# Shorter GpSimd operations, a first group without GpSimd arithmetic, later row sums and a separate bank in the last group, in a one-core decoder trunk step

## The chip, the cores and the metric

The kernel runs on one core of one Trainium2 chip. A core has five engines that run their own instruction queues and wait for one another by semaphores: TensorE (PE, matmuls, with PEld for its weight loads), VectorE (DVE), ScalarE (ACT), GpSimd (POOL) and SyncE (SP, which issues the transfers here). The metric is the device time of one execution in microseconds; a kernel's number is the median of its runs.

## The reference

One layer of a decoder trunk for 256 prompt tokens and 32 sample tokens (8 sequences of 4), T = 288 tokens in all, D = 2048 channels, float32:

```python
h = rmsnorm(x, norm1_g)
proj = h @ w_in + b_in                      # 2048 -> 3072: a, gate, z of 1024 each
u = a * sigmoid(gate)
c = silu(layernorm(depthwise_causal_conv([history, u], conv_w) + conv_b))   # 31 taps
d = window_mean([history, z], windows 2, 4, 8, 16) - z                       # one window per group of 256
p = (d @ pool_w, group by group) * pool_scale
x = x + concat(c, p) @ w_out
h2 = rmsnorm(x, norm2_g)
x = x + square(relu(h2 @ w_ff1)) @ w_ff2    # 2048 -> 8192 -> 2048
y = rmsnorm(x, norm_f)
```

The last 30 rows of u and the last 15 rows of z are outputs as well.

## The kernel before

Channels lie on the 128 partitions, the 288 tokens along the free dimension. Every weight block of 1024 x 256 values (1 MB, tile `wr`, three buffers) is loaded by SyncE and split by `split` into two halves of 128 x 1024 values; each half becomes a rounded part `whi` (ScalarE, L224) and a remainder `wlo` = wr - whi (L225, VectorE or GpSimd), with four buffers for each. The activations are split in the same way (`hx`, `dx`, `px`, `mx`, `ax`, `fx`). `gemm` multiplies in three matmuls for each k and each of two column blocks m: whi times high part (L247), whi times low part (L248), wlo times high part (L249), into `ac`, a tile of two PSUM banks, of which there are two.

Which engine makes a `wlo` is counted in eighths by `SHARE`: `turn` grows by the share of the stage at each half, and at eight the half goes to GpSimd. In the first group the halves are cut into two pieces of 128 x 512 columns (`cut=2`), in all others a piece is the whole half.

The stages are: a first group (`conv_products(0)`) for which also x is loaded and split into `hx` (L265 on ScalarE, L266 on VectorE); a second (`conv_products(1)`); five more conv groups; four pool groups (`pool_group`, windows 16, 8, 4, 2); the last conv group; then four small products with `pool_w`, the output projection over `px` (L450) and over `mx` (L459), and four rounds of the two feed-forward products (L494, L507). Each group of w_in has 96 matmuls.

The row sums of x squared are taken while the first group runs: GpSimd squares three pairs of channel blocks (L298), ScalarE five (L300), GpSimd adds (L302, L304). `rsqrt_sums` multiplies the totals by ones (`pt`, L186), takes the square root and its reciprocal; `spread` (`pr`, L204) brings it to all partitions and ScalarE copies it to `rb` (L391). In the second group's `gemm` the first is called at k = 3 and the second at k = 8.

`conv_pair` scales the product by `rb` (`ag`, L322), takes the sigmoid, writes u (L327) and then, at lowest priority (`later`), does 31 taps of the convolution one after another on VectorE, one operand in PSUM (`pc`, L337), with the sample tokens on GpSimd (`prd`, L340) and VectorE (L342); after every second channel block GpSimd adds into `sum_c` (L345, L347). `pool_group` scales (`tz`, L358), forms window sums on GpSimd by doubling (`s`, L366, 840 columns at a time), and the differences on VectorE (L369, L374, L378, L379, `dx` L382).

The order of the instructions on each engine is fixed before the run: the framework takes the program's order as priority and lets each engine take the first instruction that is ready by its own estimate of the times.

In the last feed-forward product the final group is computed with `m_outer=True`, first all k of m = 0, then all of m = 1; its product is added to x (L507), squared (L512) and added to the row sum `ssf` (L514), before the last normalisation (L524).

Of the kernel before, what the change touches and what calls it, by code (L numbers as in the profile page):

```python
# [9 lines left out]
F32 = mybir.dt.float32  # L10
F32R = mybir.dt.float32r
AF = mybir.ActivationFunctionType
ALU = mybir.AluOpType
# [4 lines left out]
D = 2048  # L18
SEQ = 256
NB, NS = 8, 4  # L20
T = SEQ + NB * NS
# [59 lines left out]
def trunk_kernel(ctx: ExitStack, tc: tile.TileContext, io):  # L81
# [18 lines left out]
    def nm(s):  # L100
        seen[s] = seen.get(s, 0) + 1
        return f"{s}{seen[s]}"
# [109 lines left out]

    def split(raw, share=0, cut=4):

        parts = []
        for h in range(2):
            hi = wspl.tile([P, 4, 256], F32R, name=nm("whi"), tag="whi")
            lo = wspl.tile([P, 4, 256], F32R, name=nm("wlo"), tag="wlo")
            turn["n"] += share
            eng = nc.gpsimd if turn["n"] >= 8 else nc.vector  # L220
            turn["n"] %= 8
            for k in range(0, 4, cut):
                src = raw[:, 4 * h + k : 4 * h + k + cut, :]
                nc.scalar.copy(hi[:, k : k + cut, :], src)  # L224
                eng.tensor_tensor(lo[:, k : k + cut, :], src, hi[:, k : k + cut, :].bitcast(F32), op=ALU.subtract)  # L225
            parts.append((hi, lo))

        def get(k, m):
            hi, lo = parts[k // 4]
            return hi[:, k % 4, m * P : (m + 1) * P], lo[:, k % 4, m * P : (m + 1) * P]  # L230

        return get

    def gemm(banks, rhs, m_outer=False, between={}):


        n = len(rhs)
        gets = ready.pop()
        order = [(k, m) for k in range(n) for m in range(2)]
        if m_outer:  # L240
            order.sort(key=lambda km: km[1])
        for k, m in order:
            if m == 0 and k in between:
                between[k]()
            (xh, xl), b = rhs[k], banks[:, m, :T]
            wh, wl = gets[k // 8](k % 8, m)
            nc.tensor.matmul(b, wh, xh, start=k == 0, stop=False)  # L247
            nc.tensor.matmul(b, wh, xl, start=False, stop=False)  # L248
            nc.tensor.matmul(b, wl, xh, start=False, stop=k == n - 1)  # L249
        ready.extend(itertools.islice(weights, 1))  # L250

    def bank2():
        return acc.tile([P, 2, 512], F32, name=nm("ac"), tag="ac")

    def halves(x2):

# [32 lines left out]

    scratch = z_all[:].rearrange("p k t -> p (k t)")[:, 0 : 5 * 2 * T].rearrange("p (n k t) -> p n k t", n=5, t=T)  # L290
    tot = [scratch[:, 0], scratch[:, 1]]
    used = [False, False]
    for q in range(8):
        xq = xT[:, 2 * q : 2 * q + 2, :]
        a = 0 if q in (0, 2, 4) else 1
        dst = scratch[:, 2 if a == 0 else 3 + q % 2] if used[a] else tot[a]
        if a == 0:
            nc.gpsimd.tensor_tensor(dst, xq, xq, op=ALU.mult)  # L298
        else:
            nc.scalar.activation(dst, xq, AF.Square)  # L300
        if used[a]:
            nc.gpsimd.tensor_tensor(tot[a], tot[a], dst, op=ALU.add)  # L302
        used[a] = True
    nc.gpsimd.tensor_tensor(tot[1], tot[1], tot[0], op=ALU.add)  # L304
    rb = row("rb")


# [3 lines left out]
    def conv_products(i, **kw):  # L311
        nc.sync.dma_start(u_all[:, i, UO:UL], io["hist_c"][:, i, :])
        bk = bank2()
        gemm(bk, hx, **kw)
        return bk

    def conv_pair(i, bk):
        up = u_all[:, i, 0:UO]
        us = samples(u_all[:, i, UO:UL], US)
        ag = tmpp.tile([P, 2, T], F32, name=nm("ag"), tag="ag", bufs=2)  # L320
        ta, tg = ag[:, 0, :], ag[:, 1, :]
        nc.vector.tensor_tensor(ag, bk[:, :, :T], both(rb), op=ALU.mult)  # L322
        nc.scalar.activation(tg, tg, AF.Sigmoid, bias=v("b_in", 8 + i))
        if i == N8 - 1:
            load_table(AF.Sqrt, tg[:, 0:1])
        for out, a, b in ((up[:, CH:UO], ta[:, :SEQ], tg[:, :SEQ]), (us[:, :, CH:US], samples(ta[:, SEQ:T], NS), samples(tg[:, SEQ:T], NS))):
            nc.vector.scalar_tensor_tensor(out=out, in0=a, scalar=v("b_in", i), in1=b, op0=ALU.add, op1=ALU.mult)  # L327
        if i % 2 == 0:
            cs.append(actp.tile([P, 2, T], F32, name=nm("c"), tag="c", bufs=4))
        c = cs[i // 2][:, i % 2, :]  # L330
        with later():
            pc = cvp.tile([P, SEQ], F32, name=nm("pc"), tag="cv", padded_shape=[P, 512])
            cwv = vec[:, CWO + i * CW : CWO + (i + 1) * CW]
            nc.scalar.activation(pc, up[:, 0:SEQ], AF.Identity, bias=v("conv_b", i), scale=cwv[:, 0:1])
            for w in range(1, CW):
                dst = pc if w < CW - 1 else c[:, 0:SEQ]
                nc.vector.scalar_tensor_tensor(out=dst, in0=up[:, w : w + SEQ], scalar=cwv[:, w : w + 1], in1=pc, op0=ALU.mult, op1=ALU.add)  # L337
            prd = prdp.tile([P, NB, NS, CW], F32, name=nm("prd"), tag="prd", padded_shape=[P, NB, NS, CW])
            for t in range(NS):
                nc.gpsimd.tensor_tensor(prd[:, :, t, :], us[:, :, t : t + CW], cwv[:, None, :].to_broadcast([P, NB, CW]), op=ALU.mult)  # L340
            cso = c[:, SEQ:T]
            nc.vector.tensor_reduce(samples(cso, NS), prd, axis=AX.X, op=ALU.add)  # L342
            nc.scalar.activation(cso, cso, AF.Identity, bias=v("conv_b", i))
            if i == 3:
                nc.gpsimd.tensor_tensor(sum_c, cs[0], cs[1], op=ALU.add)  # L345
            elif i % 2 and i > 3:
                nc.gpsimd.tensor_tensor(sum_c, sum_c, cs[i // 2], op=ALU.add)  # L347


    dd = {}  # L350
# [1 line left out]
    def pool_group(g):  # L352
        nc.sync.dma_start(z_all[:, 2 * g : 2 * g + 2, ZO:ZL], io["hist_p"][:, 2 * g : 2 * g + 2, :])
        bk = bank2()
        gemm(bk, hx)
# [13 lines left out]
        nc.vector.scalar_tensor_tensor(  # L369
# [2 lines left out]
        for m in range(2):  # L372
# [10 lines left out]
        dd[g] = halves((dh, dl))  # L383

    first = conv_products(0)
    diag = []
    second = conv_products(
        1,
        between={
            3: lambda: diag.append(rsqrt_sums([tot[1][:, 0, :], tot[1][:, 1, :]], 1.0 / D, AF.Sigmoid)),  # L390
            8: lambda: nc.scalar.copy(rb, spread(diag[0])[:, :T]),  # L391
        },
    )
    nc.gpsimd.memset(z_all[:, :, 0:PH], 0.0)
# [12 lines left out]
    mixp = {}  # L407
    for g in GROUPS:
        bk = bank2()
        gemm(bk, dd[g])  # L410
        for m, (mh, ml) in enumerate(halves(act2("px"))):
            i = 2 * g + m
            nc.scalar.activation(mh, bk[:, m, :T], AF.Copy, scale=v("pool_scale", i))
            nc.vector.scalar_tensor_tensor(out=ml, in0=bk[:, m, :T], scalar=v("pool_scale", i), in1=f32(mh), op0=ALU.mult, op1=ALU.subtract)
            mixp[i] = (mh, ml)
# [29 lines left out]

    for g in range(8):
        bk = bank2()
        gemm(bk, [mixp[k] for k in korder])
        x2 = xT[:, 2 * g : 2 * g + 2, :]
        nc.vector.tensor_tensor(x2, x2, bk[:, :, :T], op=ALU.add)  # L450

# [2 lines left out]
    ss2 = row("ss2")  # L454
    for g in range(8):
        bk = bank2()
        gemm(bk, mixc)
# [26 lines left out]
    for ch in range(DFF // FCH):  # L484
        fx = []
        for g in range(FCH // 256):
            bk = bank2()
            gemm(bk, x1)
            if ch == 0 and g == 0:
                nc.scalar.copy(r2, rsqrt_rows([ss2, q2], 1.0 / D)[:, :T])  # L490
            t = tmpp.tile([P, 2, T], F32, name=nm("t"), tag="ag", bufs=2)
            nc.vector.scalar_tensor_tensor(out=t, in0=bk[:, :, :T], scalar=0.0, in1=both(r2), op0=ALU.max, op1=ALU.mult)
            f = tmpp.tile([P, 2, T], F32, name=nm("f"), tag="ag2", bufs=2)
            nc.scalar.activation(f, t, AF.Square)  # L494
            fh, fl = act2("fx")
            nc.scalar.copy(fh, f)
            nc.vector.tensor_tensor(fl, f, f32(fh), op=ALU.subtract)
            fx += halves((fh, fl))
        last = ch == DFF // FCH - 1
        for g in range(8):  # L500
            bk = bank2()
            gemm(bk, fx, m_outer=last and g == 7)
            for m in range(2):
                k = 2 * g + m
                xk = xT[:, k, :]
                if last:
                    nc.vector.tensor_tensor(xk, xk, bk[:, m, :T], op=ALU.add)  # L507
# [76 lines left out]
```

## Time and profile before

| | us |
|---|---|
| median of 3 runs (1132.56 to 1134.32) | 1134.06 |
| the profiled execution | 1131.78 |
| its span, first to last instruction | 1130.0 |
| TensorE busy | 1092.2 (97%) |
| VectorE busy | 657.0 (58%) |
| ScalarE busy | 468.6 (41%) |
| GpSimd busy | 190.0 (17%) |

Durations in the profile come from one execution. A row of a timeline gives start, duration, engine, line, operation, output and inputs, size and count, and in brackets the idle time before it and what ended it. A row of a group gives the count, the total busy time, the mean in ns, and the idle time before. An instruction that has begun but waits for a port counts as busy. The granted clock of TensorE has a mean of 0.986 over the execution.

### The profile page before, as it was taken

Reading aid. Unit: us, or ns where it says so; the run is one execution under the profiler, and the core shown is the slowest. Engines: PE = TensorE matmul, PEld = TensorE weight load, DVE = VectorE, ACT = ScalarE, POOL = GpSimd, SP = SyncE. Lnnn points to the kernel's source line nnn. Section 1 sums busy time; section 2 is a strip of 40 time slices with the busy share of each in tenths; the row PEclk is TensorE's granted clock in tenths of the full one; section 3 lists DMA queues with packets and bytes.
Section 4 is the critical chain, followed back from the end, with each engine's and each line's share of the span. In section 5 each row is a group of like instructions: output and inputs, shape, how many; then the busy total and the mean of one; then the engine's idle time right before and its main releaser. Section 6 shows DMA issues by size and latency. Waiting matters only on the chain.

```text
span 1130.0 us, 19074 instructions
## 1 busy us (share of the span) xinstructions
PE 1092.2 (97%) x8208; PEld 1086.9 (96%) x8208; DVE 657.0 (58%) x822; ACT 468.6 (41%) x575; POOL 190.0 (17%) x139
## 2 busy tenths in 40 slices
PE   5999995999999999999999999999999999999995
PEld 5999995999999999999999999999999999999995
DVE  7699999677854454444544444455444444454553
ACT  6444444365544443333444333344433334444441
POOL 7598985431300000000000000000000000000000
PEclk9999998899999999999999999999999999999997
DMA  7554536445444444444454545454445454545432
GB/s 278 177 182 154 182 115 175 152 150 186 152 162 171 161 176 160 176 159 178 154 182 156 180 155 182 153 184 153 183 153 184 153 183 152 184 151 185 152 112 84
DMA packets 31909, 187.00 MB, mean 165 GB/s; under 512 B 3408, under 2 KB 7760, under 8 KB 10448
## 3 DMA queue, kind: packets, MB, share of 16 engines
q1 hardware_dynamic: 31680, 185.73, 47.5%
q8 instruction: 64, 1.05, 0.4%
q14 instruction: 21, 0.17, 0.0%
q10 hardware_dynamic: 144, 0.05, 0.0%
HBM read 181.49 MB, written 4.28 MB: 164 GB/s over the span
## 4 chain that ended last, share of the span: by engine, by line
PE 91%; DVE 6%; ACT 0%; issue 0%; DVEq 0%; ACTq 0%
PE ac L247 31%; PE ac L248 30%; PE ac L249 30%; DVE pc L337 2%; DVE wlo L225 1%; PE pt L186 0%; DVE xT L524 0%; DVE d L369 0%; DVE d L374 0%; DVE e L378 0%; PE pr L204 0%; DVE d L379 0%; DVE dx L382 0%; DVE c L342 0%; DVE tz L358 0%
## 5 line engine op out<-in xcount | busy, mean ns | idle before, releaser
L224 ACT CAST whi<-wr 128x1024 fp32r<-128x1024 f32 (+1 forms) x342 | 355.2, 1040 | 577.6 <-PE ac L248 569.0
L225 DVE TENSOR_TENSOR wlo<-wr,whi 128x1024 fp32r<-128x1024 f32 (+1 forms) x295 | 367.9, 1247 | 349.1 <-ACT whi L224 348.1
L247 PE MATMUL ac<-ax,whi 128*128 128x288 f32 x1024 | 302.7, 296 | 0.0
L247 PE MATMUL ac<-fx,whi 128*128 128x288 f32 x1024 | 302.4, 295 | 0.0
L248 PE MATMUL ac<-fx,whi 128*128 128x288 f32 x1024 | 301.4, 294 | 0.0
L248 PE MATMUL ac<-ax,whi 128*128 128x288 f32 x1024 | 301.3, 294 | 0.0
L249 PE MATMUL ac<-ax,wlo 128*128 128x288 f32 x1024 | 298.1, 291 | 0.0
L249 PE MATMUL ac<-fx,wlo 128*128 128x288 f32 x1024 | 298.0, 291 | 0.0
L249 PEld LDWEIGHTS ac<-fx,wlo 128*128 128x128 f32 x1024 | 192.9, 188 | 0.0
L249 PEld LDWEIGHTS ac<-ax,wlo 128*128 128x128 f32 x1024 | 192.8, 188 | 0.0
L247 PEld LDWEIGHTS ac<-ax,whi 128*128 128x128 f32 x1024 | 192.2, 188 | 0.1
L247 PEld LDWEIGHTS ac<-fx,whi 128*128 128x128 f32 x1024 | 192.2, 188 | 0.0
L248 PEld LDWEIGHTS ac<-ax,whi 128*128 128x128 f32 x1024 | 192.0, 187 | 0.1
L248 PEld LDWEIGHTS ac<-fx,whi 128*128 128x128 f32 x1024 | 192.0, 187 | 0.0
L249 PE MATMUL ac<-hx,wlo 128*128 128x288 f32 x384 | 115.8, 302 | 12.4 <-DVE wlo L225 11.6
L225 POOL TENSOR_TENSOR wlo<-wr,whi 128x1024 fp32r<-128x1024 f32 (+1 forms) x47 | 112.4, 2402 | 51.0 <-ACT whi L224 50.8
L247 PE MATMUL ac<-hx,whi 128*128 128x288 f32 x384 | 115.8, 302 | 0.3 <-ACT whi L224 0.3
L248 PE MATMUL ac<-hx,whi 128*128 128x288 f32 x384 | 113.9, 297 | 0.0
L337 DVE SCALAR_TENSOR_TENSOR pc<-u_all,vec,pc 128x256 f32<-128x256 f32 x232 | 99.1, 482 | 3.5 <-issue 1.2
L249 PEld LDWEIGHTS ac<-hx,wlo 128*128 128x128 f32 x384 | 73.5, 191 | 14.3 <-DVE wlo L225 13.1
L247 PEld LDWEIGHTS ac<-hx,whi 128*128 128x128 f32 x384 | 73.9, 192 | 0.8 <-ACT whi L224 0.8
L248 PEld LDWEIGHTS ac<-hx,whi 128*128 128x128 f32 x384 | 73.8, 192 | 0.3
(111 smaller groups left out, 844.4 us busy)
## 6 DMA issues: line engine op xcount, KB each, us to landing
wr<-in_w SPq DMA_DIRECT2D x167, 1024.0 KB, 4.9
xT<-in_xT SPq DMA_DIRECT2D x8, 288.0 KB, 5.9
wr<-in_w SPq DMA_DIRECT2D x8, 256.0 KB, 5.7
out_u_out<-u_all SPq DMA_DIRECT2D x1, 1208.0 KB, 9.0
out_yT<-xT SPq DMA_DIRECT2D x2, 576.0 KB, 2.9
u_all<-in_hist_c SPq DMA_DIRECT2D x8, 136.0 KB, 4.8
out_z_out<-z_all SPq DMA_DIRECT2D x1, 668.0 KB, 8.9
z_all<-in_hist_p SPq DMA_DIRECT2D x4, 152.0 KB, 4.3
```

The source lines that it names most:

```text
L224: nc.scalar.copy(hi[:, k : k + cut, :], src)
L225: eng.tensor_tensor(lo[:, k : k + cut, :], src, hi[:, k : k + cut, :].bitcast(F32), op=ALU.subtract)
L247: nc.tensor.matmul(b, wh, xh, start=k == 0, stop=False)
L248: nc.tensor.matmul(b, wh, xl, start=False, stop=False)
L249: nc.tensor.matmul(b, wl, xh, start=False, stop=k == n - 1)
L337: nc.vector.scalar_tensor_tensor(out=dst, in0=up[:, w : w + SEQ], scalar=cwv[:, w : w + 1], in1=pc, op0=ALU.mult, op1=ALU.add)
```

## The change

Four edits. `SHARE["first"]` goes from 2 to 0, so that no `wlo` of the first group is made on GpSimd. Where GpSimd makes a `wlo`, it does so in pieces of two k-blocks, 512 columns; the window sums and the channel sums are cut into one operation for each m as well. The squares of x all go to ScalarE and their additions to VectorE, in program order behind the first group's product and the second group's weights, with two totals of two parts each that `pt` adds up; `pt` is called at k = 10 of the second group and the spread at k = 14. In the last group of the last product, m = 1 accumulates in a bank of another tile.

```diff
-SHARE = {"first": 2, "second": 4, "conv": 7, "pool": 5, "pool_w": 3, "w_out": 6}
+SHARE = {"first": 0, "second": 4, "conv": 7, "pool": 5, "pool_w": 3, "w_out": 6}
...
             turn["n"] += share
-            eng = nc.gpsimd if turn["n"] >= 8 else nc.vector
+            slow = turn["n"] >= 8
             turn["n"] %= 8
             for k in range(0, 4, cut):
                 src = raw[:, 4 * h + k : 4 * h + k + cut, :]
                 nc.scalar.copy(hi[:, k : k + cut, :], src)
-                eng.tensor_tensor(lo[:, k : k + cut, :], src, hi[:, k : k + cut, :].bitcast(F32), op=ALU.subtract)
+                eng, step = (nc.gpsimd, 2) if slow else (nc.vector, cut)
+                for j in range(k, k + cut, step):
+                    eng.tensor_tensor(lo[:, j : j + step, :], raw[:, 4 * h + j : 4 * h + j + step, :], hi[:, j : j + step, :].bitcast(F32), op=ALU.subtract)
...
-    used = [False, False]
-    for q in range(8):
-        xq = xT[:, 2 * q : 2 * q + 2, :]
-        a = 0 if q in (0, 2, 4) else 1
-        dst = scratch[:, 2 if a == 0 else 3 + q % 2] if used[a] else tot[a]
-        if a == 0:
-            nc.gpsimd.tensor_tensor(dst, xq, xq, op=ALU.mult)
-        else:
+
+    def squares():
+        for q in range(8):
+            xq = xT[:, 2 * q : 2 * q + 2, :]
+            a = q // 4
+            dst = scratch[:, 2 + q % 3] if q % 4 else tot[a]
             nc.scalar.activation(dst, xq, AF.Square)
-        if used[a]:
-            nc.gpsimd.tensor_tensor(tot[a], tot[a], dst, op=ALU.add)
-        used[a] = True
-    nc.gpsimd.tensor_tensor(tot[1], tot[1], tot[0], op=ALU.add)
+            if q % 4:
+                nc.vector.tensor_tensor(tot[a], tot[a], dst, op=ALU.add)
...
-            if i == 3:
-                nc.gpsimd.tensor_tensor(sum_c, cs[0], cs[1], op=ALU.add)
-            elif i % 2 and i > 3:
-                nc.gpsimd.tensor_tensor(sum_c, sum_c, cs[i // 2], op=ALU.add)
+            if i % 2 and i > 1:
+                for m in range(2):
+                    nc.gpsimd.tensor_tensor(sum_c[:, m, :], (cs[0] if i == 3 else sum_c)[:, m, :], cs[i // 2][:, m, :], op=ALU.add)
...
-            nc.gpsimd.tensor_tensor(s2[:, :, 2 * w - 1 :], s[:, :, 2 * w - 1 :], s[:, :, w - 1 : ZL - w], op=ALU.add)
+            for m in range(2):
+                nc.gpsimd.tensor_tensor(s2[:, m, 2 * w - 1 :], s[:, m, 2 * w - 1 :], s[:, m, w - 1 : ZL - w], op=ALU.add)
...
     first = conv_products(0)
+    squares()
     diag = []
     second = conv_products(
         1,
         between={
-            3: lambda: diag.append(rsqrt_sums([tot[1][:, 0, :], tot[1][:, 1, :]], 1.0 / D, AF.Sigmoid)),
-            8: lambda: nc.scalar.copy(rb, spread(diag[0])[:, :T]),
+            10: lambda: diag.append(rsqrt_sums([t[:, m, :] for t in tot for m in range(2)], 1.0 / D, AF.Sigmoid)),
+            14: lambda: nc.scalar.copy(rb, spread(diag[0])[:, :T]),
         },
     )
...
-            gemm(bk, fx, m_outer=last and g == 7)
+            banks = each(bk)
+            if last and g == 7:
+                banks[1] = bank2()[:, 1, :]
+            gemm(banks, fx, m_outer=last and g == 7)
...
-                    nc.vector.tensor_tensor(xk, xk, bk[:, m, :T], op=ALU.add)
+                    nc.vector.tensor_tensor(xk, xk, banks[m][:, :T], op=ALU.add)
```

More of the change, by code (lines that the diff above doesn't have):

```diff
@@ L253, in bank2, with each @@
         return acc.tile([P, 2, 512], F32, name=nm("ac"), tag="ac")
+    def each(bk):
+        return [bk[:, m, :] for m in range(2)]
     def halves(x2):
@@ L313, in conv_products @@
         bk = bank2()
-        gemm(bk, hx, **kw)
+        gemm(each(bk), hx, **kw)
         return bk
@@ L354, in pool_group @@
         bk = bank2()
-        gemm(bk, hx)
+        gemm(each(bk), hx)
         z = z_all[:, 2 * g : 2 * g + 2, :]
@@ L409, in trunk_kernel @@
         bk = bank2()
-        gemm(bk, dd[g])
+        gemm(each(bk), dd[g])
         for m, (mh, ml) in enumerate(halves(act2("px"))):
@@ L447, in trunk_kernel @@
         bk = bank2()
-        gemm(bk, [mixp[k] for k in korder])
+        gemm(each(bk), [mixp[k] for k in korder])
         x2 = xT[:, 2 * g : 2 * g + 2, :]
@@ L456, in trunk_kernel @@
         bk = bank2()
-        gemm(bk, mixc)
+        gemm(each(bk), mixc)
         x2 = xT[:, 2 * g : 2 * g + 2, :]
@@ L487, in trunk_kernel @@
             bk = bank2()
-            gemm(bk, x1)
+            gemm(each(bk), x1)
             if ch == 0 and g == 0:
```

2 lines of the change are left out of this document (1 added, 1 removed).

## The prediction

> **What bounds the kernel now.** I read first the busy time by stage, because the share over the whole span hides the stages (busy time of each engine in four stretches; PE is TensorE, DVE VectorE, ACT ScalarE, POOL GpSimd, with the count of instructions behind each).
>
> ```profile
> 6.00:36.00 30.00, 18.05 (x100) 15.92 (x99) 26.66 (x23) 16.18 (x31) 19.81 (x12) 0.89 0.79 290
> 45.00:200.00 155.00, 143.18 (x1044) 141.68 (x1044) 150.03 (x293) 66.52 (x96) 128.32 (x78) 0.97 0.50 160
> 130.00:200.00 70.00, 58.18 (x402) 56.68 (x401) 67.25 (x122) 29.09 (x46) 52.55 (x27) 0.93 0.54 157
> 250.00:1114.00 864.00, 864.00 (x6590) 863.89 (x6589) 435.95 (x425) 352.30 (x403) 13.40 (x14) 1.00 0.47 163
> ```
>
> From 250 on TensorE never pauses: 864/6590 = 0.1311 us a matmul. Nothing in the change touches that rate. At that rate the 100 matmuls of 6 to 36 need 13.1 of 30 us, and the 402 of 130 to 200 need 52.7 of 70. So 16.9 us are lost in the first group and 17.3 in the pool stage, where VectorE is busy 67.25 of 70. Everything the change can win lies in these two places and in the tail. The waits of TensorE say who ends them:
>
> ```profile
> PE ac L249 <- DVE wlo L225: 11.6, 6, 3.9
> PE ac L247 <- ACT whi L224: 4.8, 2, 4.5
> PE ac L247 <- DVE px L414: 3.3, 2, 3.1
> PE ac L247 <- DVE ag L322: 3.3, 1, 3.3
> ```
>
> The first row is the first group, the others the pool stage; the rest of the loss is matmuls at the reduced clock after a pause (granted 0.89 and 0.93 in these stretches). Next, why VectorE is late: its timeline, then GpSimd's.
>
> ```profile
> 6.17 0.69 DVE L225 TENSOR_TENSOR wlo<-wr,whi 128x512 fp32r<-128x512 f32 x1
> 6.85 0.95 DVE L266 SCALAR_TENSOR_TENSOR hx<-xT,vec,hx 128x288 fp32r<-128x288 f32 x2
> 8.82 0.69 DVE L225 TENSOR_TENSOR wlo<-wr,whi 128x512 fp32r<-128x512 f32 x1 [1.03 <-ACT whi L224]
> ...
> 13.90 3.27 DVE L266 SCALAR_TENSOR_TENSOR hx<-xT,vec,hx 128x288 fp32r<-128x288 f32 x2
> 17.10 1.88 DVE L225 TENSOR_TENSOR wlo<-wr,whi 128x512 fp32r<-128x512 f32 x1
> ...
> 45.07 0.76 DVE L322 TENSOR_TENSOR ag<-ac,rb 128x576 f32<-128x576 f32 x1 [1.68 <-ACT rb L391]
> ```
>
> ```profile
> 13.40 6.86 POOL L302 TENSOR_TENSOR z_all<-z_all 128x576 f32<-128x576 f32 x4
> ```
>
> The same pair of hx costs 0.95 us while GpSimd is idle and 3.27 beside its sums; wlo goes from 0.69 to 1.88. A VectorE operation with two SBUF operands waits for the GpSimd operation in flight to end. The conv step, whose second operand is in PSUM, does not show it: 482 ns on average over 210, in the first row below.
>
> ```profile
> L337 DVE SCALAR_TENSOR_TENSOR pc<-u_all,vec,pc 128x256 f32<-128x256 f32 x210 | 88.4, 482 | 3.0 <-issue 1.2 <-ACT pc L334 1.1
> L225 DVE TENSOR_TENSOR wlo<-wr,whi 128x1024 fp32r<-128x1024 f32 x11 | 17.9, 1627 | 1.0 <-ACT whi L224 1.0
> L327 DVE SCALAR_TENSOR_TENSOR u_all<-ag,vec 128x256 f32<-128x256 f32 (+1 forms) x16 | 9.9, 657 | 0.6 <-ACT ag L323 0.6
> ...
> L369 DVE SCALAR_TENSOR_TENSOR d<-s,z_all 128x482 f32<-128x482 f32 (+3 forms) x4 | 4.8, 1208 | 0.0
> L374 DVE SCALAR_TENSOR_TENSOR d<-s,z_all 128x32 f32<-128x32 f32 x8 | 4.8, 636 | 0.0
> L378 DVE TENSOR_TENSOR e<-s,rcnt 128x30 f32<-128x30 f32 (+3 forms) x4 | 4.3, 1076 | 0.0
> ```
>
> These are VectorE's groups from 40 to 200. What the same operations take when nothing is in their way:
>
> ```profile
> 79.29 0.64 DVE L327 SCALAR_TENSOR_TENSOR u_all<-ag,vec 128x256 f32<-128x256 f32 x2
> ...
> 185.21 0.68 DVE L369 SCALAR_TENSOR_TENSOR d<-s,z_all 128x510 f32<-128x510 f32 x1
> 185.81 0.29 DVE L374 SCALAR_TENSOR_TENSOR d<-s,z_all 128x32 f32<-128x32 f32 x2
> ```
>
> Taking 1.23 for a free wlo (an estimate from 0.69 for half the columns, less a fixed 0.15), the waits are 17.9-11x1.23 = 4.4, 9.9-8x0.64 = 4.8, 4.8-4x0.68 = 2.1, 4.8-4x0.29 = 3.6 and, with 0.15 for a free L378 (half the L374 pair), 4.3-0.6 = 3.7: together 18.6 us of VectorE's time between 40 and 200.
>
> **The first group without GpSimd.** The change takes GpSimd's ten two-operand operations for the sum of squares out of this stage, and gives the last two of the eight wlo steps (SHARE 0) to VectorE. What is left on VectorE is eight times a hx pair and a wlo: 8x(0.95+0.69) = 13.1 us. It starts at 5.0, since the wlo at 6.17 follows its hx pair directly, and loses the 1.03 us that the row at 8.82 shows for the second piece: last wlo done at 19.1, less about 0.2 that successive rows overlap (6.85 starts when 0.68 of the 0.69 is over): 18.9. The transfers bear it:
>
> ```profile
> 10.92 0.33 SPq L154 DMA_DIRECT2D wr<-in_w  x1
> wr<-in_w SPq DMA_DIRECT2D x8, 256.0 KB, 5.7
> ```
>
> The last of the eight pieces is issued at 10.92 and takes about 5.7 us: 16.6, ahead of its turn. After the last wlo some 10 matmuls remain, 1.3 us: the group ends at 20.2. Before:
>
> ```profile
> 29.67 0.61 PE L249 MATMUL ac<-hx,wlo 128*128 128x288 f32 x1 [3.92 <-DVE wlo L225]
> ...
> 38.14 1.10 PE L186 MATMUL pt<-ones,z_all 128*96 128x1 f32 x12
> ```
>
> The row-sum matmul pt stood 3 k-steps, 18 matmuls (2.4 us), into the second group, so the first ended at 35.8. TensorE is 15.6 us earlier.
>
> **The sums, later.** All eight squares go to ACT and six adds to VectorE, during the second group; pt moves from k=3 to k=10 and the spread to k=14. An add of 576 columns is priced by the ag row, 0.76: 4.6 us, and up to the length of a GpSimd operation more for each. VectorE had little to do there, so I cost the adds at zero; their deadline is k=10, 20.2+60x0.1311 = 28.1, with VectorE and ACT free of the first group from 19 on. If the cover fails, pt stalls TensorE by what they are late. Two things the move does cost. The totals stay four parts instead of two, so pt has twice the matmuls of the row at 38.14: about 1.0 us more on TensorE, which is then 14.6 us earlier. And rb comes 84 matmuls after the start of group two, plus 2.0 for pt, plus an estimated 1.1 from the spread to ag: 20.2+11.0+2.0+1.1 = 34.3 instead of 45.07. So the conv work on VectorE starts 10.8 us earlier.
>
> **Operations of 512 columns.** From 45 to 200 GpSimd runs 34 wlo halves, ten window sums and the channel sums. The prices, from GpSimd's groups by shape:
>
> ```profile
> L225 POOL TENSOR_TENSOR wlo<-wr,whi 128x1024 fp32r<-128x1024 f32 x45 | 109.5, 2442 | 51.0 <-ACT whi L224 50.8
> ...
> L225 POOL TENSOR_TENSOR wlo<-wr,whi 128x512 fp32r<-128x512 f32 x2 | 2.9, 1488 | 0.0
> L347 POOL TENSOR_TENSOR sum_c<-sum_c,c 128x576 f32<-128x576 f32 x2 | 2.9, 1438 | 0.2 <-DVE c L337 0.2
> ```
>
> A line through 1024 and 576 columns gives 2.24 ns a column and 0.147 us fixed, so a piece of 512 takes 1.295 and a half 2.59: 0.15 more, 5.0 us for 34 halves, 1.5 for the window sums. The other bound is the 512 row itself, 1488 ns: 2.98 a half, 0.53 more, 18 us for 34. I take the first, because the two 512 pieces ran while hx was contending. GpSimd idles 155-128.3 = 26.7 us in this stretch, which covers 6.5, so the cost is zero. The Trainium skill's GPSIMD Engine Reference (section 3.1) speaks against the cut: every instruction pays two software hops and a join on the slowest of eight cores; its 4497 ns for 2048 columns beside our 2442 would make an estimated fixed part of 0.39 us and 13 us for 34 halves, still inside the idle time; it raises the chance of the last rival below.
>
> In return, a waiting VectorE operation waits for a piece about half as long: of 18.6 us about half is saved, 9.3. The bounds are zero (a wait at every piece) and the whole 18.6. The skill's SBUF — State Buffer ("Who interferes with whom") has the same lock, held for the whole instruction; the hx rows agree, and by that rule the remainder is halved while the port time is not.
>
> In 130 to 200 VectorE sets the pace, so its gains add: 10.8 + 9.3 = 20.1 us. TensorE arrives 14.6 earlier, and of the 17.3 it loses there 17.3+14.6-20.1 = 11.8 remain.
>
> **Two banks for the last group.** Its first half's add and square no longer wait for the last matmul. Before:
>
> ```profile
> 1114.58 0.82 DVE L507 TENSOR_TENSOR xT<-xT,ac 128x288 f32<-128x288 f32 x2 [9.47 <-PE ac L249]
> 1115.54 0.46 DVE L514 TENSOR_TENSOR ssf<-ssf,q 128x288 f32<-128x288 f32 x1
> ```
>
> The ssf add of 0.46 leaves the path, with 0.04 around it: 0.5. The second tile must be free of group six's adds, which ended half a group (6.3 us) earlier: no cost.
>
> **Sum:** 10.8 + 9.3 + 0.5 = 20.6 us. The profiled execution took 1131.8 us, span 1130.0, so 1111.2; the median of the runs, 1134.06, is 2.3 above it, so 1113.5.
>
> **Rivals.**
> - *Shorter pieces save nothing*: VectorE, in order, meets a GpSimd piece as often and as long in sum. Only 10.8+0.5 remain: 1122.8. For it: GpSimd is busy 83% of 45 to 200, so pieces follow one another. Against: a pair of tiny L374 operations costs 0.29 free and 1.2 on average, which is one GpSimd operation's remainder each.
> - *The sums do not move*: the order on each engine is planned from estimated times, and the adds may be put into the first group. VectorE then needs 4.6 us more there: 1134.1-(6.2+9.3+0.5) = 1118.1.
> - *VectorE stops being the bound*: all stalls of the pool stage vanish, 14.6+17.3+0.5 = 32.4: 1101.7. For it: conv steps can be put off to after 200, where VectorE idles. Against: 67.25 of 70 is far from that.
> - *Slower, the port is used up*: in the conv and pool stages GpSimd becomes the bound. At 1488 ns a piece it needs 18 us more for the halves, and by the same ratio (0.53x840/1024 = 0.43 each) 5.6 for ten window and three channel sums: 23.3. If in-order waits for whi keep its 26.7 us of idle from being used, all of it comes on the path and the saved waits are worth nothing: 23.3-10.8-0.5 = +12.0, 1146.1. It turns slower when over 11.3 of the 23.3 are on the path.
>
> **How the numbers follow.** A measurement of this kernel tells about 0.2% (2.3 us) from no change. Chances: the forecast 0.43, pieces save nothing 0.20 (0.02 of it with other losses down to no change), sums in the first group 0.12, VectorE no longer the bound 0.15, port used up 0.10. Faster 0.88, same 0.02, slower 0.10. The range takes in 1101.7, rounded down to 1101, at the low end and, at the high end, shorter pieces worth nothing with the sums in the first group, 6.2+0.5: 1127.4, so 1128.
>
> **What would show it.** Right: no hx pair of VectorE above 1.0 us in the first group and its last wlo near 19; pt near 29; the first ag near 34; GpSimd pieces near 1.3 us; L374 pairs near half of their 1.2 us; TensorE losing some 12 us in the pool stage; one DVE step fewer between the last matmul and pt. Wrong: GpSimd pieces at 1.5 us and TensorE waiting for POOL wlo through the conv groups; adds or squares between the first group's wlo; pt stalled by the adds; VectorE's waits in the pool stage as large as before.

## The result, and the profile after

The changed kernel takes 1121.61 us (median of four, 1121.02 to 1122.98) beside 1134.19 for the kernel before on the same chip: a ratio of 0.9894, 95% interval 0.9877 to 0.9911. It gains 12.6 us, inside the range that was forecast and on the side that was forecast, and 8 us short of the 20.6 that the sum gave. By the time alone two rivals of the prediction stand nearer (1122.8 and 1118.1) than its sum (1113.5), so the traces have to decide. Repeated later, the changed kernel took 1122.58 beside 1131.70, a gain of 9.1. The profiled execution took 1121.02, its span 1119.2; against the span of 1130.0 before that is 10.8, and the traces are accounted for on this number.

First the stages of the kernel after (length, busy time of PE, PEld, DVE, ACT and POOL with counts, granted clock, DMA share, GB/s):

```profile
6.00:36.00 30.00, 28.37 (x209) 26.83 (x209) 21.32 (x39) 22.73 (x39) 9.38 (x8) 1.00 0.98 358
36.45:185.00 148.55, 139.41 (x1018) 138.16 (x1017) 146.39 (x290) 64.82 (x95) 137.18 (x122) 0.97 0.50 162
130.00:200.00 70.00, 60.86 (x418) 59.50 (x418) 66.89 (x129) 31.21 (x49) 57.97 (x48) 0.93 0.54 162
410.00:1090.00 680.00, 680.00 (x5146) 680.00 (x5145) 326.08 (x309) 264.92 (x287) 0.00 (x0) 1.00 0.47 164
```

In 6 to 36 TensorE now runs 182 matmuls of the products where it ran 98 (the 209 and 100 of the rows count the row sums, the spread and the warm-up too). From 130 to 200 there are 418 instead of 402: at 0.1311 us each 54.8 us, so 15.2 are still lost there (17.3 before). The last row has something new, read against the same stretch of the kernel before:

```profile
410.00:1090.00 680.00, 680.00 (x5189) 680.00 (x5188) 328.77 (x311) 266.28 (x287) 0.00 (x0) 1.00 0.48 168
```

TensorE does not pause in either, yet it gets through 43 fewer matmuls: 680/5189 = 0.1310 us each before, 680/5146 = 0.1321 after. Over the 6144 matmuls of the feed-forward stage this is 6.7 us that the changed kernel gives back, in a stage whose code the change leaves alone.

When TensorE reached each product shows the rest. The rows give the matmuls of the output projection over `px` (the end of the VectorE-bound stretch) and over `mx`; the start is the first number after the shortest, median and longest duration. Before, then after:

```profile
L247 PE MATMUL ac<-px,whi x128: 292/298/510, 200.8 to 256.0; 128*128 128x288 f32 x128
L247 PE MATMUL ac<-mx,whi x128: 294/296/298, 256.4 to 306.8; 128*128 128x288 f32 x128
```

```profile
L250 PE MATMUL ac<-px,whi x128: 293/295/442, 185.0 to 239.2; 128*128 128x288 f32 x128
L250 PE MATMUL ac<-mx,whi x128: 294/296/298, 239.6 to 290.0; 128*128 128x288 f32 x128
```

So 15.8 us are won up to `px` and 16.8 up to `mx`. From there to the last matmul 6.7 are lost by the pace, and the tail is 0.7 shorter: 16.8 - 6.7 + 0.7 = 10.8.

VectorE at the start, after:

```profile
4.98 0.95 DVE L272 SCALAR_TENSOR_TENSOR hx<-xT,vec,hx 128x288 fp32r<-128x288 f32 x2 [3.98 <-ACT hx L271]
...
8.00 0.76 DVE L306 TENSOR_TENSOR z_all<-z_all 128x576 f32<-128x576 f32 x1
...
20.20 0.75 DVE L306 TENSOR_TENSOR z_all<-z_all 128x576 f32<-128x576 f32 x1
20.87 1.82 DVE L228 TENSOR_TENSOR wlo<-wr,whi 128x512 fp32r<-128x512 f32 x2
22.99 0.16 DVE L188 TENSOR_SCALAR st<-pt 96x3 f32<-96x3 f32 x1 [0.30 <-PE pt L186]
...
36.45 0.76 DVE L325 TENSOR_TENSOR ag<-ac,rb 128x576 f32<-128x576 f32 x1 [5.61 <-ACT rb L395]
37.61 0.76 DVE L325 TENSOR_TENSOR ag<-ac,rb 128x576 f32<-128x576 f32 x1 [0.40 <-PE ac L252]
```

Every hx pair takes 0.94 or 0.95. But the six adds of the sum of squares (the first and the last are shown) were put between the pieces of the first group, and the last of the eight `wlo` ends at about 21.5 (the row at 20.87 holds it and the second group's first, of 1024 columns). The second `ag`, which waits for group two's last matmul, comes at 37.6 instead of 50.2. The first comes at 36.5 instead of 45.1, after VectorE has idled 5.61 us for `rb`. TensorE's longest wait in 6 to 40, and then the two longest in 130 to 200:

```profile
PE ac L252 <- DVE wlo L228: 1.3, 5, 0.4
...
PE ac L250 <- DVE px L418: 5.2, 2, 4.0
PE ac L252 <- DVE wlo L228: 3.8, 1, 3.8
```

The 11.6 us of waits of the first group are 1.3 now; in the pool stage it is still VectorE that ends them. VectorE's groups there (38 to 200), and two of GpSimd's operations with nothing in their way, then its group of wlo:

```profile
L228 DVE TENSOR_TENSOR wlo<-wr,whi 128x1024 fp32r<-128x1024 f32 x12 | 18.9, 1577 | 0.0
L330 DVE SCALAR_TENSOR_TENSOR u_all<-ag,vec 128x256 f32<-128x256 f32 (+1 forms) x16 | 11.7, 768 | 0.3 <-ACT ag L326 0.3
L377 DVE SCALAR_TENSOR_TENSOR d<-s,z_all 128x32 f32<-128x32 f32 x8 | 6.4, 804 | 0.0
...
L372 DVE SCALAR_TENSOR_TENSOR d<-s,z_all 128x482 f32<-128x482 f32 (+3 forms) x4 | 3.7, 925 | 0.0
...
L381 DVE TENSOR_TENSOR e<-s,rcnt 128x30 f32<-128x30 f32 (+3 forms) x4 | 0.6, 161 | 0.0
```

```profile
34.94 2.53 POOL L228 TENSOR_TENSOR wlo<-wr,whi 128x512 fp32r<-128x512 f32 x2 [0.58 <-ACT whi L225]
...
L228 POOL TENSOR_TENSOR wlo<-wr,whi 128x512 fp32r<-128x512 f32 x74 | 98.1, 1358 | 14.9 <-ACT whi L225 14.9
```

By the prediction's free prices the waits in these five rows are 18.9-12x1.23 = 4.1, 11.7-8x0.64 = 6.6, 6.4-4x0.29 = 5.2, 1.0 and 0: 16.9 us, where they were 18.6. The tail, last:

```profile
1104.47 0.45 DVE L514 TENSOR_TENSOR xT<-xT,ac 128x288 f32<-128x288 f32 x1 [4.92 <-PE ac L252]
1106.50 0.16 DVE L188 TENSOR_SCALAR st<-pt 96x3 f32<-96x3 f32 x1 [1.58 <-PE pt L186]
```

One add follows the last matmul instead of two, and no `ssf` step lies between it and `pt`, as was said.

### The profile page after: what moved, and what is told of

It reads as the page before. It is cut to its first block, busy times and chain, and to the rows that moved or that the text cites. A ratio compares the mean times of both kernels' runs of the same rounds, so it can differ in the third digit from the quotient of the medians.

```text
span 1119.2 us, 19178 instructions
## 1 busy us (share of the span) xinstructions
PE 1095.0 (98%) x8220; PEld 1090.7 (97%) x8220; DVE 646.2 (58%) x830; ACT 470.1 (42%) x578; POOL 185.8 (17%) x185
## 4 chain that ended last, share of the span: by engine, by line
PE 93%; POOL 2%; DVE 2%; DMA 1%; ACT 1%; issue 1%; SPq 0%; DVEq 0%; ACTq 0%; POOLq 0%
PE ac L250 31%; PE ac L252 31%; PE ac L251 30%; POOL wlo L228 1%; POOL s L369 1%; DMA wr<-in_w 1%; PE pt L186 0%; DMA xT<-in_xT 0%; DVE xT L531 0%; ACT whi L225 0%; ACT hx L271 0%; PE pr L204 0%; DVE px L418 0%; DVE hx L272 0%; DVE pc L340 0%
## 5 line engine op out<-in xcount | busy, mean ns | idle before, releaser
L228 DVE TENSOR_TENSOR wlo<-wr,whi 128x1024 fp32r<-128x1024 f32 (+1 forms) x297 | 364.0, 1226 | 352.2 <-ACT whi L225 351.3
L252 PE MATMUL ac<-ax,wlo 128*128 128x288 f32 x1024 | 301.8, 295 | 0.0
L252 PE MATMUL ac<-fx,wlo 128*128 128x288 f32 x1024 | 301.8, 295 | 0.0
L228 POOL TENSOR_TENSOR wlo<-wr,whi 128x512 fp32r<-128x512 f32 x90 | 119.4, 1358 | 48.1 <-ACT whi L225 48.1
```

Of the source, the lines that this page charges most:

```text
L228: eng.tensor_tensor(lo[:, j : j + step, :], raw[:, 4 * h + j : 4 * h + j + step, :], hi[:, j : j + step, :].bitcast(F32), op=ALU.subtract)
```

## The experiments

**The parts by themselves.** The kernel before was run once more, for how much one trace differs from the next.

> The kernel before, unchanged, profiled on the chip of the next three runs. In the changed kernel a matmul of the feed-forward stage took 0.1322 us (100 us hold 758 of them) against 0.1311 (765) before, 6.5 us over the stage. If that pace belongs to the chip of the profiled execution, this run shows 758 too where its neighbours do; if it belongs to the kernel, it shows 765 and the span 1130 again.

It took 1131.22 us; first `ag` at 46.1, `px` at 201.0, `mx` at 255.8. It ran the feed-forward stage at the faster pace (536 matmuls in 410 to 480), and so did two of its three neighbours, but not the third, so the pace doesn't belong to the chip. Its two traces differ by 1.0 us at the first `ag`, 0.2 at `px` and 0.6 at `mx`. Three traces of the changed kernel's code (two of the kernel, one of it with an addition that stands behind `mx`, below) lie further apart: `px` at 185.0, 187.2 and 184.7, `mx` at 239.6, 241.3 and 240.1. So a difference of 2 us between two traces tells little.

The next kernel has all of the change but the shorter operations and the second bank:

```diff
-                eng, step = (nc.gpsimd, 2) if slow else (nc.vector, cut)
+                eng, step = (nc.gpsimd, cut) if slow else (nc.vector, cut)
...
-            for m in range(2):
-                nc.gpsimd.tensor_tensor(s2[:, m, 2 * w - 1 :], ...)
+            nc.gpsimd.tensor_tensor(s2[:, :, 2 * w - 1 :], ...)
```

> Only the first group's part of the change (no GpSimd share there, squares and sums on ScalarE and VectorE, row sums called later); GpSimd operations of the full size as before, one tile in the last group. Theory A (the shorter pieces are worth nothing, the first group is the whole gain): ratio within 0.4% of the changed kernel's 0.989, about 1119 to 1124 us. Theory B (the pieces pay by shorter waits of VectorE, as predicted, 9 us): about 1130 us. Theory C (the pieces cost GpSimd time that is on the path): below 1117 us.

It took 1124.7 us, 0.9949 of before (0.9934 to 0.9964). The time is near Theory A's range, but this trace ran the feed-forward stage at the faster pace (536 matmuls in 410 to 480) and that of the changed kernel at the slower (532), so the two times can't be compared as they stand. The other one adds to the kernel before only the shorter operations:

```diff
-                eng.tensor_tensor(lo[:, k : k + cut, :], src, ...)
+                step = 2 if eng is nc.gpsimd else cut
+                for j in range(k, k + cut, step):
+                    eng.tensor_tensor(lo[:, j : j + step, :], ...)
```

> Only the pieces: GpSimd's wlo of 1024 columns in two operations of 512, window and channel sums one operation for each m; first group, sums and last group as before. Theory A: 1131 to 1136 us, no change. Theory B: 1124 to 1126. Theory C: 1138 or more. In the first group the hx pairs of VectorE stay above 2.5 us in all three, since the squares are still on GpSimd.

It took 1131.99, 1.0006 of before (0.9994 to 1.0018): by the time, nothing. The traces say otherwise. The product over `px` and over `mx` in the first kernel, then in the second:

```profile
L250 PE MATMUL ac<-px,whi x128: 294/295/509, 192.1 to 248.5; 128*128 128x288 f32 x128
L250 PE MATMUL ac<-mx,whi x128: 295/295/296, 248.9 to 298.9; 128*128 128x288 f32 x128
```

```profile
L249 PE MATMUL ac<-px,whi x128: 292/295/402, 195.7 to 249.2; 128*128 128x288 f32 x128
L249 PE MATMUL ac<-mx,whi x128: 294/296/298, 249.6 to 299.9; 128*128 128x288 f32 x128
410.00:1090.00 680.00, 680.00 (x5145) 680.00 (x5144) 325.43 (x307) 263.86 (x284) 0.00 (x0) 1.00 0.48 166
```

Against the repeated kernel before, the first group alone brings 8.9 us at `px` and 6.9 at `mx`, the shorter operations alone 5.3 and 6.2; beside the first group they bring 7.1 and 9.3 (192.1 to 185.0, 248.9 to 239.6). (Beside the repeated trace of the changed kernel it is 4.9 and 7.6.) The two by themselves sum to 14.2 and 13.1, and both in one kernel bring 16.0 and 16.2 (13.8 and 14.5 by the repeated trace): as far as these traces tell, the two gains add up. The kernel with the shorter operations alone reached `mx` 6.2 us earlier and then ran the feed-forward stage at the slower pace (its last row), which took 6.7 back. So the time alone would have led to the wrong verdict on this part.

What the shorter operations take away is seen between the two kernels that start alike (first `ag` at 36.7 and 36.5). VectorE's rows of the kernel without them, 38 to 200, and its stretch from first `ag` to `px`:

```profile
L228 DVE TENSOR_TENSOR wlo<-wr,whi 128x1024 fp32r<-128x1024 f32 x11 | 20.5, 1864 | 0.0
L330 DVE SCALAR_TENSOR_TENSOR u_all<-ag,vec 128x256 f32<-128x256 f32 (+1 forms) x16 | 11.3, 742 | 0.3 <-ACT ag L326 0.3
L375 DVE SCALAR_TENSOR_TENSOR d<-s,z_all 128x32 f32<-128x32 f32 x8 | 9.2, 1183 | 0.0
...
L370 DVE SCALAR_TENSOR_TENSOR d<-s,z_all 128x482 f32<-128x482 f32 (+3 forms) x4 | 4.2, 1062 | 0.0
...
L379 DVE TENSOR_TENSOR e<-s,rcnt 128x30 f32<-128x30 f32 (+3 forms) x4 | 2.9, 715 | 0.0
...
36.67:192.10 155.43, 140.88 (x1017) 138.79 (x1016) 154.23 (x292) 64.50 (x94) 124.53 (x77) 0.97 0.49 156
```

The same sum gives 7.0 + 6.2 + 8.0 + 1.5 + 2.3 = 25.0 us of waits. The first group's edit has raised them by 6.4 over the 18.6 of before, and the shorter operations lower them by 8.1, to 16.9. In the kernel with the shorter operations alone the same five groups (40 to 200: 18.7 for twelve, 11.6, 6.6, 3.6 and 0.6) make 16.7: without the early start they lower the waits by 1.9 only, and the stretch from first `ag` (43.6) to `px` by 2.8, from 154.9 in the repeated kernel before to 152.1. The stretch of the kernel before was

```profile
45.07:200.80 155.73, 143.91 (x1047) 142.41 (x1046) 150.62 (x294) 66.48 (x95) 128.25 (x78) 0.97 0.51 161
```

VectorE idled 5.1 us of it, 1.2 in the kernel without shorter operations and 2.2 after. So the early start reached `px` undiminished (8.4 us at the first `ag`, 45.07 to 36.67, and 8.7 at `px`): the longer waits went into idle time. Between before and after the stretch is 7.2 us shorter, of which 2.9 is idle time and 4.2 busy time; of the busy time 1.7 are four convolution steps fewer (214 instead of 218, the others run later) and 1.7 the waits of the five rows.

**Which half of the first group's edit does it.** One kernel takes the kernel before and only sets the share; the other is the changed kernel with the old share.

```diff
-SHARE = {"first": 2, ...}
+SHARE = {"first": 0, ...}
```

> The kernel before with only the share of the first group set to 0: all eight wlo steps of the first group on VectorE, the squares and sums still half on GpSimd. Theory A1 (the squares on GpSimd are what slows the first group, each hx of VectorE waits for one of them): hx pairs still above 2.5 us beside the squares, first group no earlier than 33, 1130 to 1136 us. Rival A2 (the share is the gain): first group ends before 28, below 1127 us.

1133.72 us, 1.0014 (0.9998 to 1.003). First `ag` at 41.0, and in the trace the hx pairs at 9.3 and 13.8 still take 3.00 and 3.27 us. The time and the pairs are as Theory A1 has them, but the first group ended near 30.0 (`pt` starts at 32.4, 18 matmuls later), not after 33: the share alone brings 5.8 us there and 4 to 5 at the first `ag`, of which little arrives.

```profile
L247 PE MATMUL ac<-px,whi x128: 294/296/445, 198.7 to 255.2; 128*128 128x288 f32 x128
L247 PE MATMUL ac<-mx,whi x128: 295/296/297, 255.6 to 305.6; 128*128 128x288 f32 x128
```

```diff
-SHARE = {"first": 0, ...}
+SHARE = {"first": 2, ...}
```

> The changed kernel with the first group's share back at 2: the last two of the eight wlo pieces go to GpSimd, squares and sums stay on ScalarE and VectorE. Theory A1: the first ag within 1 us of the changed kernel's 36.4 and the first product at the pool stage's end (px) within 2 us of 185.0; VectorE's last hx pair waits for up to two pieces of 1.3 us. Rival A2: first ag 3 us later or more. The time itself is 1121 or, at the other pace of TensorE, 1114.5.

1123.62 us, 0.9929 (0.9906 to 0.9952); first `ag` at 39.7, `px` at

```profile
L250 PE MATMUL ac<-px,whi x128: 293/296/428, 188.9 to 242.7; 128*128 128x288 f32 x128
```

With the share at 0 and without shorter operations, moving the squares and adds off GpSimd is worth 6.6 us at `px` (198.7 to 192.1); with them moved and the operations short, the share is worth 3.9 (188.9 to 185.0; 1.7 beside the other trace of the changed kernel, 187.2). The first `ag` is 3.2 later than in the changed kernel, so Rival A2 of this run holds. By itself, with the squares left on GpSimd, the share is worth 2.3 there and nothing at `mx` (255.6 beside 255.8). So the squares are the larger half by these traces, and the share pays, if at all at `px`, once they are gone.

**The 5.61 us before the first ag.** The trace of after has `pt` done at 23.0, the diagonal that the spread reads at 26.2, and the spread only at 35.3, where k = 14 puts it. Two kernels call the two earlier, at k = 2 and 6, and at k = 0 and 2:

```diff
-            10: lambda: diag.append(rsqrt_sums(...)),
-            14: lambda: nc.scalar.copy(rb, spread(diag[0])[:, :T]),
+            2: lambda: diag.append(rsqrt_sums(...)),
+            6: lambda: nc.scalar.copy(rb, spread(diag[0])[:, :T]),
```

> The changed kernel with the row sums called at k=2 and the spread at k=6 of the second group instead of 10 and 14 (the spread stands 48 matmuls, 6.3 us, earlier in TensorE's order). In the changed kernel VectorE is idle 5.6 us until the first ag at 36.4, while the diagonal it waits for is done at 26.2. Theory A (VectorE sets the pace to the end of the pool stage): first ag near 30, and 4 to 6 us less, 1116 to 1118. Rival D (GpSimd, busy 9.6 of 10 from 46 to 166, or the planned order sets it): 1120 to 1123.

> Row sums called at k=0 and the spread at k=2 of the second group: the spread stands 12 matmuls (1.6 us) ahead of its place in the early-spread kernel, whose diagonal was done at 27.0 and whose first ag was at 31.0. Theory A (VectorE sets the pace): first ag near 29.4 and px and mx up to 1.6 us earlier. Rival D (planned order or GpSimd sets it): no change within 1 us. Time 1112 to 1115, or 6.8 more at the other pace.

The first took 1114.11 us, 0.985 of before (0.9831 to 0.9868), the second 1117.42, 0.9864 (0.9837 to 0.9891). The first `ag` came at 31.0 and 29.2, 5.5 and 7.3 us earlier than after. The rows of the first of them:

```profile
L250 PE MATMUL ac<-px,whi x128: 290/295/510, 183.8 to 239.1; 128*128 128x288 f32 x128
L250 PE MATMUL ac<-mx,whi x128: 294/296/298, 239.5 to 289.9; 128*128 128x288 f32 x128
410.00:1090.00 680.00, 680.00 (x5188) 680.00 (x5188) 328.98 (x314) 266.68 (x291) 0.00 (x0) 1.00 0.47 164
```

`px` starts 1.2 us earlier and `mx` at the same time as after; in the second kernel they start at 183.9 and 238.3. Beside the other two traces of the changed kernel's code `px` is 0.9 and 3.4 earlier. So the idle time before the first `ag` was for the most part not on the path: an earlier start of the conv work was taken up in the stretch that follows, from first `ag` to `px` 152.8 us instead of 148.5. VectorE is busy for 4.9 us more of it (151.3 instead of 146.4), 1.9 of them for five more convolution steps, which the changed kernel does later. By `px` and `mx` that is Rival D's outcome, by the first `ag` Theory A's; what takes up the rest isn't shown. The first of these kernels is the fastest of all, 7.5 us below after, but by the pace: its feed-forward stage ran at 5188 matmuls per 680 us.

**The size of GpSimd's operations**, on the kernel with the early spread: 1024 and 256 columns for wlo instead of 512 (the window and channel sums stay cut by m).

```diff
-                eng, step = (nc.gpsimd, 2) if slow else (nc.vector, cut)
+                eng, step = (nc.gpsimd, cut) if slow else (nc.vector, cut)   # 1024
+                eng, step = (nc.gpsimd, 1) if slow else (nc.vector, cut)     # 256
```

> The early-spread kernel with GpSimd's wlo back in one operation of 1024 columns; window and channel sums stay cut. Read at the first px and mx matmul (183.8 and 239.5 with 512), which the two paces of TensorE do not touch. Theory B (a waiting VectorE operation waits about half a GpSimd operation): VectorE's waits in 30 to 200 grow by 5 to 9 us and px and mx come 5 to 9 us later. Theory A (the size is worth nothing): within 2 us of 183.8 and 239.5.

> The early-spread kernel with GpSimd's wlo in four operations of 256 columns. Theory B with a fixed cost of some 0.1 us a piece (two uncontended pieces of 512 took 2.55 us, one of 1024 2.40): GpSimd needs some 0.3 us more for each half, 10 us for 34, and is busy all of 50 to 130; VectorE's waits shrink by 3 to 5 us. px and mx between 3 us earlier and 3 us later than 183.8 and 239.5. Rival E (the port is used up): px and mx 5 us or more later, TensorE waiting for GpSimd's wlo in the conv groups.

With 1024 it took 1128.68 us, 0.9963 (0.9943 to 0.9982); with 256, 1141.62, 1.007 (1.0043 to 1.0097). `mx` with 1024, then with 256, whose waits of TensorE in 130 to 260 and whose GpSimd group are shown too:

```profile
L250 PE MATMUL ac<-mx,whi x128: 294/296/298, 247.4 to 297.8; 128*128 128x288 f32 x128
```

```profile
L250 PE MATMUL ac<-mx,whi x128: 294/296/298, 259.5 to 309.9; 128*128 128x288 f32 x128
PE ac L250 <- ACT dx L384: 14.0, 2, 8.2
L228 POOL TENSOR_TENSOR wlo<-wr,whi 128x256 fp32r<-128x256 f32 x138 | 102.8, 782 | 6.1 <-ACT whi L225 3.7 <-DMA wr<-in_w 2.4
```

`px` starts at 190.0 for 1024, 183.8 for 512 and 196.8 for 256, `mx` at 247.4, 239.5 and 259.5: far more than two traces of one kernel differ by. A piece of 256 takes 782 ns on average, so a half takes 3.13 us against 2.72 (2x1358) and 2.49 whole (that kernel's mean). GpSimd is then busy for 150.5 of the 166 us from first `ag` to `px`, 10.3 more than with 512, and TensorE waits 14.0 us for `dx`, which is made from GpSimd's window sums. The kernel ends slower than before, as the prediction's last rival has it. But its mechanism isn't shown: GpSimd is busy for 91% of the stretch and was for 92% with 512 (140.2 of 152.8), and the wait that the prediction named (TensorE for POOL wlo) is not the one that shows. The trace is of an execution of 1134.2 us; the median is 1141.6.

The positions came as the two texts said (Theory B for 1024, Rival E for 256), the waits of VectorE did not. Over 30 to 200 the five rows make 18.1 us with 512, 19.6 with 1024 instead of 5 to 9 more, and 19.8 with 256 instead of 3 to 5 less. So the size of the pieces is worth what the positions say, and the five rows alone don't account for it.

**The pace.** The changed kernel was run once more as it is, and once with a small disturbance: one more matmul of 128 columns ahead of each of the four feed-forward rounds, into a tile that nothing reads.

```diff
         fx = []
+        nudge = ms("nudge")
+        nc.tensor.matmul(nudge[:, 0:P], ones, ones, start=True, stop=True)
```

> The changed kernel again. So far a matmul of the feed-forward stage took 0.1311 us in the kernel before (two profiles), in the first group alone and with the early spread, and 0.1322 in the changed kernel and with the pieces alone, with the same instructions in the same order; 6144 of them make 6.8 us. Theory S (a state into which TensorE's stream falls after its last pause, which small differences of time decide): the executions of this one kernel fall into two groups some 6.8 us apart, near 1114.5 and 1121.2. Rival K (it belongs to the kernel): all within 2 us of 1121.5.

> The changed kernel with one small extra matmul (128 columns, of ones, result unused) ahead of each of the four feed-forward rounds. Theory S: the pace differs between the four rounds of one profile, or is 0.1311 in some (765 matmuls in 100 us instead of 758), and the time is between 1114.5 and 1122. Rival K (whatever makes the stream slow stands in the kernel): 758 to 759 in all four rounds and 1122 us.

Again: 1122.58 us, 0.9919 (0.9905 to 0.9934), `mx` at 241.3 and 5145 matmuls in 410 to 1090, the slower pace; its four executions lie within 1.4 us, which is Rival K's outcome. With the nudges: 1118.39, 0.9883 (0.9867 to 0.9899). Its stretches of 70 us; the nudges stand at 290.9, 494, 697 and 899.1:

```profile
410.00:480.00 70.00, 70.00 (x536) 70.00 (x535) 31.28 (x28) 23.29 (x23) 0.00 (x0) 1.00 0.48 168
510.00:580.00 70.00, 70.00 (x532) 70.00 (x531) 34.73 (x33) 29.42 (x32) 0.00 (x0) 1.00 0.47 166
...
710.00:780.00 70.00, 70.00 (x536) 70.00 (x535) 36.06 (x34) 31.20 (x35) 0.00 (x0) 1.00 0.48 168
...
1010.00:1080.00 70.00, 70.00 (x536) 70.00 (x535) 36.67 (x46) 32.76 (x47) 0.00 (x0) 1.00 0.46 165
```

Rounds one, three and four run at 536 matmuls in 70 us (0.1306), round two at 532 (0.1316; a short window counts the matmuls at its edges and reads a little low): the pace changes at the second and the third nudge and holds between, inside one execution, at a granted clock of 1.00 throughout. It changes without a nudge too. In the kernel before, the row-sum matmuls `pt` of the second normalisation stand at 319.9; the 60 us ahead of them and 60 us behind:

```profile
257.00:317.00 60.00, 60.00 (x456) 60.00 (x455) 44.16 (x44) 31.95 (x52) 13.40 (x14) 1.00 0.47 163
330.00:390.00 60.00, 60.00 (x460) 60.00 (x459) 31.76 (x31) 26.44 (x30) 0.00 (x0) 1.00 0.49 171
```

In the kernel with the share alone it is the other way round, 460 and then 456. So the pace is no property of the feed-forward code: it can change where other small matmuls stand in the stream.

## Why the prediction was right, and where its sum was off

The forecast of 20.6 us is what was measured plus three differences: 10.8 + 3.3 (16.8 instead of 20.1 up to `mx`) + 6.7 (the pace) - 0.2 (the tail, 0.7 instead of 0.5). The direction and the two places of the gain were right by mechanism; the sizes were off as follows.

*First group.* Its mechanism holds: no pair of hx waits, TensorE's waits fall from 11.6 to 1.3, and group two ends 12.6 us earlier (forecast 14.6), the first `ag` is 8.6 earlier (10.8). The step that failed is "their deadline is k=10 ... with VectorE and ACT free of the first group from 19 on": the adds were not held back but put between the wlo of the first group, which is the second rival's mechanism, six times 0.75 = 4.5 us. The last wlo ended at 21.5 instead of 18.9, so 2.6 later: one add fell into the 1.03 us of waiting that the sum had charged, and successive rows overlap by more than the 0.2 that it allowed. `pt` started at 21.2, not 29, ahead of the first group's last ten matmuls. Nothing stalled for it, and the loss was 2 us instead of that rival's 4.6. Setting the spread at k = 14 put the first `ag` at 36.5 although all it needed was there earlier; by the run with the spread at k = 6 this cost 1.2 us at `px` and nothing at `mx`, no more than two traces differ by.

*Shorter operations.* The price of a piece held: 2.53 for two, 1.27 each beside 1.295 forecast, 0.13 to 0.15 for a further instruction, as a whole half of the kernel before took 2.38 with VectorE idle (at 37.0) and 2.40 (at 44.4). The prediction's estimate of 0.39 from the Trainium skill's GPSIMD Engine Reference (section 3.1) was too high; the trace decides. The step that was mis-sized is "of 18.6 us about half is saved, 9.3". Taken from the kernel before, the cut saves 1.9 us of these waits and 5.3 at `px`. It saves 8.1, 7.1 at `px` and 9.3 at `mx`, beside the first group's edit, which had first raised the waits to 25.0; that the 9.3 comes out there is in part luck. "Its gains add" holds (14.2 as the sum of the two by themselves, 13.8 to 16.0 together at `px`). "VectorE sets the pace", the reason given for it, holds in part: the waits of TensorE in the pool stage are VectorE's, but a start 5.5 us earlier brought only 1.2 at `px`. From before to after the waits fell by 1.7 only, and the observation that was to show the step right, the L374 pair at half of its 1.2 us, came out the other way: its successor L377 went from 636 to 804 ns each. The same pairs by their rows, before and then after (shortest, median and longest, or the mean, in ns):

```profile
L374 DVE SCALAR_TENSOR_TENSOR d<-s,z_all x8: 180/188/2395, 144.9 to 185.9; 128x32 f32<-128x32 f32 x8
L327 DVE SCALAR_TENSOR_TENSOR u_all<-ag,vec 128x32 f32<-128x32 f32 x8 | 1.9, 242 | 0.0
```

```profile
L377 DVE SCALAR_TENSOR_TENSOR d<-s,z_all x8: 179/872/1281, 135.5 to 173.8; 128x32 f32<-128x32 f32 x8
L330 DVE SCALAR_TENSOR_TENSOR u_all<-ag,vec 128x32 f32<-128x32 f32 x8 | 4.0, 500 | 0.0
```

Before, six of the eight tiny operations ran free (180 to 193) and two waited, 1581 and 2395, so the prediction's "one GpSimd operation's remainder each" was an average over pairs that waited and pairs that didn't. After, the longest wait is about a piece, but seven of the eight wait: the two of a pair stood back to back before (144.88 and 146.39) and stand apart in the new order (135.47 and 138.03), so each meets GpSimd by itself. Of the second operations of the `u_all` pairs none waited before (239 to 247) and two of eight do after (1276 and 1282). The waits that did shrink are those of single operations: `e<-s` from 4.3 us to 0.6 for four, L369 from 4.8 to 3.7. The Trainium skill's SBUF — State Buffer (section "Who interferes with whom") has the lock held for the whole instruction; the rows agree, with 2395 at most beside operations of 2.4 us and 1282 beside pieces of 1.3.

*What TensorE loses in the pool stage.* Forecast 11.8 of 17.3 left, measured 15.2 in 130 to 200. The forecast took 14.6 at the start and 20.1 at the end of the stage; with the 12.6 and 15.8 that were measured its own arithmetic leaves 14.1.

*The pace.* "Nothing in the change touches that rate" was true of the code and wrong of the time. The prediction had taken 0.1311 us from one execution as a constant, and the rate has two values. That is 6.7 of the 9.8 us by which the profiled execution missed the sum.

*Rivals.* "The sums do not move" is what happened, at less than half its price. "Pieces save nothing" falls, although the time lies nearest to it (7.1 and 9.3 us between two kernels that start alike), "VectorE stops being the bound" falls (5.2 and 3.8 us of waits of TensorE for VectorE), "port used up" doesn't happen at 512 columns; at 256 its outcome does, without its mechanism being shown. (Its 23.3 should read 23.6, 18 + 5.6; nothing hangs on that.)

## What to carry to other kernels

The waits between two engines that share a port are not a fixed sum of which an edit takes its part. Here one and the same cut lowered them by 1.9 us beside a late start of VectorE's work and by 8.1 beside an early one, so cost a second edit against the kernel with the first in it. A busy engine does not by that alone set the pace: work that can be put off, as the convolution steps here, fills its time. Where GpSimd shares a port with a busy VectorE, the size of its operation has an optimum that is worth a few runs (here 512 columns: 1024 and 256 are 8 and 20 us later at the same place). And before a part is called worthless because the time stands still, look at where each stage starts, since a gain and a loss of equal size can lie in different stages.

## What the runs showed of the hardware that had not been expected

One and the same stream of matmuls, 128 x 128 weights with 288 columns, with no pause of TensorE and at a granted clock of 1.00, runs at one of two paces: 758 or 765 matmuls in 100 us. Of the profiled executions, the faster one shows in before, its repetition, the first group alone, the early spread at k = 6 with pieces of 512 and the one with 256; the slower one in all others but the nudged one, which shows both. (That is from 330 us on; ahead of the second normalisation's `pt` the pace can be the other.) Times of one kernel split by about the same 6 us in the first group alone (ten executions at 1123.7 to 1126.1 and two at 1130.7 and 1130.9), but no trace of those two was kept. The eight executions of the changed kernel lie within 2.1 us, the two that were profiled at the slower pace. That the pace can change at a single small matmul and then holds is shown; what about the instant sets it, and why the changed kernel drew the slower each time, is open. At the faster pace the changed kernel would stand at an estimated 1121.6 - 6.7 = 1114.9.
